# Two-layer MLA/SSD/pooling backbone: a fixed bias tile, an earlier band load and a new order around the pooling of layer 1

## The chip, the cores and the metric

The kernel runs on one core of one Trainium2 chip. The metric is the device time of one execution in microseconds (us). The engines are named as in the profile: PE (TensorE matmuls) and PEld (its weight loads), DVE (VectorE), ACT (ScalarE), POOL (GpSimd) and SP (SyncE). In this kernel SP only issues DMAs, and ACT issues some DMAs in between its own work, so that a DMA of ACT's that has to wait holds up ACT.

## The reference

Two layers over 640 tokens of width 1024: 128 context tokens and 512 latent tokens. Layer 0 mixes tokens by latent attention and a two-way state space scan, layer 1 by pooling with four windows. Each layer ends in a SwiGLU network (the FFN) of hidden width 2816. Shifts, scales and gates of every part come from conditioning vectors. Cut to what the change touches:

```
def modulation(cvec, w_mod, b_mod):
    m = jnp.expand_dims(jax.nn.silu(cvec) @ w_mod + b_mod, -2)
    return split_last(m, (D_MODEL,) * 6)

def modulate(x, g, shift, scale):
    return rmsnorm(x, g) * (1 + scale) + shift

def pool_mixer(h, w_pool, pool_scale):
    for gi, w in enumerate(POOL_WINDOWS):          # 2, 4, 8, 16
        lo = np.clip(t - w // 2, 0, L)
        hi = np.clip(t + w // 2, 0, L)
        ...
        outs.append(mean - hf[..., gi * POOL_GC:(gi + 1) * POOL_GC])
    out = jnp.einsum('blgc,gcd->blgd', pooled, w_pool).reshape(b, L, d)
    return out * pool_scale

def swiglu(h, w_gate, w_up, w_down):
    return (jax.nn.silu(h @ w_gate) * (h @ w_up)) @ w_down

    for l in range(DEPTH):
        ...
        xs = xs + g_s * rmsnorm(mix_s, norm_post_mix[l])
        fs = swiglu(modulate(xs, norm_pre_ffn[l], shf_s, scf_s), ffn_w_gate[l], ffn_w_up[l], ffn_w_down[l])
        xs = xs + gf_s * rmsnorm(fs, norm_post_ffn[l])
```

Outputs are the tokens after both layers, and the new latent keys and scan states of layer 0.

## The kernel before

Tokens stand in five tiles of 128: tile 0 is the context, tiles 1 to 4 the latent grid. All matmuls of the FFN split each operand into a high and a low part (h = rounded copy, l = rest) and add three products. The splits are work for other engines: ACT writes the high part (L89, L421, L589), DVE or POOL subtract to get the low part (L90, L422, L590).

The program runs in this order: layer 0's mixer (to about 475 us), FFN 0 (to about 909), the transition with the whole mixer of layer 1 (to about 990), FFN 1, and the last residual.

**FFN.** Each FFN works through 11 pairs of a gate and an up block of 256 hidden columns; each block is a `Matrix`. A matrix is multiplied with seven products in place of eight (Strassen's way): p1 to p7 (L515, with weights `a1h`, `a2h` and the like from the tokens, and `ha`, `hc`, `la`, `lc` and the like from the matrix). POOL forms the sums of quarters that this needs (`adds`, L485 to L488), ACT and DVE split them (`hw`/`lw`, `hc`/`lc`, ...). Pair 0 runs ahead (`plain`, `first`), in the plain form for what the transposed tokens allow and in the seven-product form for the rest; in the code below, `seq` holds the other 20 matrices, and each iteration of the loop over `seq` does one matrix `m`, prepares the next (`nx.load`, `nx.a`, `nx.adds`, `nx.c`, `nx.b`, `nx.d`), and, between the products, runs five tiles of the down projection of the pair before (`down_add`, L97 to L99 with weights `hw`, `lw` and the tokens' `ah`, `al`). In an iteration PE's order is p1, p2, p5, p6, two down tiles, p7, a down tile, and so on. `p6` overwrites the PSUM tile that `act`'s copy at L549 (an ACT instruction) has to have read before. `out_split` writes `ah` on ACT (L589) and `al` on POOL (L590).

**Background rows.** While an FFN runs, a generator `net.bg` computes the gates of later residuals (silu(c) times w_mod, plus b_mod) on DVE, a few instructions at each call: `mod_gate_mac` loads 512 KB pieces `mraw` and adds them up in `macc` (L275). The first addition takes the bias from a tile `bb`: zeros in all rows but the first, which holds a row of `b_mod`. POOL clears `bb` (L263), and then ACT issues the DMA of row 0 (L264). This is done for six half-gates: four in FFN 0, two in FFN 1.

**Transition.** `finish0` takes the finished FFN tiles one after the other: last down tiles on PE, sum on DVE (L612), norm and gate (L350 to L353 and L365, writing the residual `xs`), the norm of the next mixer (L311, L316, writing `hn`). From `hn`, `pool_in(tt)` computes a pooled tile on PE: the window means are a product of `hn` with a banded matrix, `band` (1056 KB), for the tile itself, with eight columns for the overlap with the tile in front and eight for the tile behind (L1354). The results go through ACT and DVE (L1361, L1359, writing `pf`, with a per-channel factor and an offset `mv`). `mix(tt)` multiplies `pf` by the pool weights (L1658) and does the residual, its norm (writing `y`) and leaves a function that transposes `y` (`tr`, L332) for FFN 1. PE's order is set by hand: `after` puts pool 0, mix 0, pool 1, mix 1 and pool 2 between the FFN tails of tiles 1 to 4, and `rest` does what is left. The offset's factor needs column sums of `band`: `_band_shift` reduces `band` on DVE to `rs` (L1369), a PE matmul with ones adds it over the partitions (L1371), and eight small DVE instructions write `mv` (L1374).

Within each engine the order of instructions is what a scheduler of the framework makes of the program; DMAs of SP and ACT stand in those engines' orders.

## Time and profile before

| | |
|---|---|
| runs | 1447.77, 1449.42, 1452.63 us; median 1449.42 |
| the profiled execution | 1448.13 us |
| its span in the trace | 1446.3 us, mean granted clock of PE 0.978 |
| PE | 1370.3 us busy (95%), 7914 matmuls |
| DVE | 984.5 us busy (68%) |
| ACT | 639.0 us busy (44%) |
| POOL | 415.9 us busy (29%) |
| DMA | 165.45 MB, 114 GB/s on average |

PE is busy nearly all the time, so the page alone says little; the timelines of single stretches show where it is not. Times in the trace start at the span's start. In rows of the timeline, the number in brackets is the idle time of that engine ahead of the instruction and what ended it. The granted clock is that of PE: 1.00 is its full level of 2.4 GHz, and a stretch at half that is 1.2 GHz. The matmuls of pooling and mixing appear as two records each.

### The profile page before, as it was taken

Reading aid. Unit: us, or ns where it says so; the run is one execution under the profiler, and the core shown is the slowest. Engines: PE = TensorE matmul, PEld = TensorE weight load, DVE = VectorE, ACT = ScalarE, POOL = GpSimd, SP = SyncE. Lnnn points to the kernel's source line nnn. Section 1 sums busy time; section 2 is a strip of 40 time slices with the busy share of each in tenths; the row PEclk is TensorE's granted clock in tenths of the full one; section 3 lists DMA queues with packets and bytes.
Section 4 is the critical chain, followed back from the end, with each engine's and each line's share of the span. In section 5 each row is a group of like instructions: output and inputs, shape, how many; then the busy total and the mean of one; then the engine's idle time right before and its main releaser. Section 6 shows DMA issues by size and latency. Waiting matters only on the chain.

```text
span 1446.3 us, 20387 instructions
## 1 busy us (share of the span) xinstructions
PE 1370.3 (95%) x7914; PEld 1172.8 (81%) x7914; DVE 984.5 (68%) x1468; ACT 639.0 (44%) x1140; POOL 415.9 (29%) x349
## 2 busy tenths in 40 slices
PE   5999999999999889999999999797899999999997
PEld 2788765576658879989989998687889989999996
DVE  3755547767836886786877865666876776666557
ACT  3544644753414644334333334467444343343433
POOL 0000034253400353424343333002533333333320
PEclk8999999989999999999999999899999999999999
DMA  9434345600063243232332325320242323222213
GB/s 371 129 124 143 117 136 196 225 15 15 30 198 122 95 144 100 85 131 88 111 115 83 116 88 177 145 88 30 96 131 88 105 81 115 88 88 88 86 46 145
DMA packets 50276, 165.45 MB, mean 114 GB/s; under 512 B 5938, under 2 KB 9522, under 8 KB 50052
## 3 DMA queue, kind: packets, MB, share of 16 engines
q1 hardware_dynamic: 43344, 153.96, 32.0%
q10 hardware_dynamic: 6836, 10.19, 2.2%
q8 instruction: 62, 1.02, 0.3%
q14 instruction: 34, 0.28, 0.1%
HBM read 155.57 MB, written 8.56 MB: 113 GB/s over the span
## 4 chain that ended last, share of the span: by engine, by line
PE 74%; DVE 10%; DMA 6%; issue 4%; ACT 3%; POOL 2%; POOLq 0%; ACTq 0%; DVEq 0%; SPq 0%
PE ps L515 26%; PE ps L97 11%; PE ps L99 11%; PE ps L98 11%; DMA mraw<-in_w_mod 3%; PE ps L179 3%; DVE macc L275 3%; PE ps L1354 2%; PE ps L1255 1%; PE ps L1658 1%; PE ps L1237 1%; DMA band<-in_band 1%; PE ps L1217 1%; PE ps L1238 1%; PE ps L1239 1%
## 5 line engine op out<-in xcount | busy, mean ns | idle before, releaser
L485 POOL TENSOR_TENSOR q<-raw,raw 128x512 f32<-128x512 f32 x40 | 54.9, 1372 | 362.7 <-DMA raw<-in_w_up 117.2
L99 PE MATMUL ps<-hw,al 128*128 128x512 f32 x380 | 151.2, 398 | 1.8 <-POOL al L590 1.8
L97 PE MATMUL ps<-hw,ah 128*128 128x512 f32 x380 | 151.5, 399 | 0.8 <-ACT ah L589 0.8
L98 PE MATMUL ps<-lw,ah 128*128 128x512 f32 x380 | 151.3, 398 | 0.0
L612 DVE TENSOR_TENSOR y<-y,ps 128x512 f32<-128x512 f32 x180 | 121.1, 683 | 39.1 <-PE ps L99 36.5
L515 PE MATMUL ps<-a2h,hc 128*128 128x320 f32 x320 | 100.8, 315 | 12.2 <-ACT sg L549 12.2
L590 POOL TENSOR_TENSOR al<-sg,ah 128x640 fp32r<-128x640 f32 x42 | 78.2, 1861 | 92.5 <-ACT ah L589 83.8
L515 PE MATMUL ps<-a2h,hb 128*128 128x320 f32 x320 | 99.5, 311 | 1.8 <-ACT sg L559 1.2
L515 PE MATMUL ps<-a2h,lc 128*128 128x320 f32 x320 | 100.1, 313 | 0.0
L515 PE MATMUL ps<-a2l,hc 128*128 128x320 f32 x320 | 100.1, 313 | 0.0
L515 PE MATMUL ps<-a1h,la 128*128 128x320 f32 x320 | 99.0, 309 | 0.2 <-DVE la L90 0.2
L515 PE MATMUL ps<-a1h,ha 128*128 128x320 f32 x320 | 98.9, 309 | 0.0
L515 PE MATMUL ps<-a1l,ha 128*128 128x320 f32 x320 | 98.8, 309 | 0.0
L515 PE MATMUL ps<-a2l,hb 128*128 128x320 f32 x320 | 98.8, 309 | 0.0
L515 PE MATMUL ps<-a2h,lb 128*128 128x320 f32 x320 | 98.8, 309 | 0.0
L275 DVE SCALAR_TENSOR_TENSOR macc<-mraw,silc,macc 128x512 f32<-128x512 f32 x84 | 79.3, 972 | 28.0 <-DMA mraw<-in_w_mod 28.0
L99 PEld LDWEIGHTS ps<-hw,al 128*128 128x128 f32 x380 | 71.9, 189 | 19.7 <-POOL al L590 2.6
L488 POOL TENSOR_TENSOR t<-raw,q 128x512 f32<-128x512 f32 x40 | 58.5, 1464 | 100.0 <-DVE ld L90 65.8
L97 PEld LDWEIGHTS ps<-hw,ah 128*128 128x128 f32 x380 | 72.4, 191 | 13.7 <-ACT ah L589 1.7
L98 PEld LDWEIGHTS ps<-lw,ah 128*128 128x128 f32 x380 | 72.2, 190 | 12.2
L89 ACT ACTIVATE hd<-t 128x512 fp32r<-128x512 f32 x40 | 25.3, 632 | 120.6 <-PE ps L515 105.9
L90 DVE TENSOR_TENSOR lc<-q,hc 128x1024 fp32r<-128x1024 f32 x40 | 48.9, 1222 | 37.5 <-ACT hc L89 37.3
(445 smaller groups left out, 3943.5 us busy)
## 6 DMA issues: line engine op xcount, KB each, us to landing
raw<-in_w_mod SPq DMA_DIRECT2D x56, 512.0 KB
raw<-in_w_gate SPq DMA_DIRECT2D x44, 512.0 KB
raw<-in_w_up SPq DMA_DIRECT2D x44, 512.0 KB
raw<-in_w_down SPq DMA_DIRECT2D x44, 512.0 KB
mraw<-in_w_mod SPq DMA_DIRECT2D x40, 512.0 KB
xs<-xd SPq DMA_DIRECT2D x10, 512.0 KB
x<-in_x_sample SPq DMA_DIRECT2D x8, 512.0 KB
raw<-in_w_xbc SPq DMA_DIRECT2D x8, 512.0 KB
```

Source lines behind the costliest of these rows:

```text
L90: (eng or self.nc.vector).tensor_tensor(l, x, h.bitcast(F32), ALU.subtract)
L97: mm(out, ah, bh, start=first and i == 0, stop=False)
L98: mm(out, ah, bl, start=False, stop=False)
L99: mm(out, al, bh, start=False, stop=last and i == n - 1)
L179: nc.tensor.matmul(out[32 * g : 32 * g + 32], self.silc[:, kc], x[:, k2 * 512 : k2 * 512 + 512], start=kc < 4, stop=kc >= 4,)
L275: nc.vector.scalar_tensor_tensor(acc[:, v], x[:, k2 * 512 : k2 * 512 + 512], self.silc[:, kc, v : v + 1], acc[:, v] if kc else bb, op0=ALU ...
L485: g.tensor_tensor(self.q[:, lo], self.rb[:, lo], self.ra[:, lo], ALU.subtract)
L488: g.tensor_tensor(self.t4, self.ra[:, hi], self.q[:, hi], ALU.subtract)
L515: mm(out, x[:, k], z[:, k], start=first and n == 0, stop=n == len(terms) - 1, skip_group_check=True)
L590: (eng or nc.gpsimd).tensor_tensor(al, g.s[:, f], ah.bitcast(F32), ALU.subtract)
L612: nc.vector.tensor_tensor(yd, yd, out, ALU.add)
L1354: nc.tensor.matmul(o, x, m, start=i == 0, stop=i == len(mats) - 1, skip_group_check=True)
```

## The change

- The bias tile `bb` is made once for each layer, cleared by DVE in front of the pair loop, and each half-gate only loads its row 0.
- In the pair loop, the splits of a matrix's b and d quarters (`m.b()`, `m.d()`) move from the iteration before into the matrix's own iteration, behind p2 and behind p6. `A.fourth()`, the last of the sums of tokens, moves into the first iteration.
- The load of `band` goes from ACT's queue to SP's, in the program behind the residuals of tiles 0 and 1. The second gate tile is loaded behind it.
- The column sums of `band` come with an input (columns 40 to 43 of `bvec`), so that the DVE reduction goes and `_band_shift` needs no band.
- The eight columns for the tile behind are left out for the first two channel chunks (the pooling window of 2 has no reach behind it).
- In `rest`, mix 2 stands ahead of pool 3, and the transposes stand elsewhere.

```
-        bb = self.mrp.tile([P, 512], F32, tag="bb", name=self.name("bb"), bufs=1)
+        bb = self.bb
...
-        nc.gpsimd.memset(bb, 0.0)
...
+    net.bb = net.mrp.tile([P, 512], F32, name=net.name("bb"))
+    nc.vector.memset(net.bb, 0.0)
...
-    n1.b()
-    n1.d()
-    A.fourth()
...
         w.p2()
+        m.b()
...
         w.p6()
+        m.d()
         if nx:
             nx.a()
         d()
+        if n == 2:
+            A.fourth()
...
-        if nx:
-            nx.b()
-            nx.d()
...
-            if 0 < tt < NT - 1:
+            if 0 < tt < NT - 1 and dc >= 2:
...
-    rs = net.small.tile([P, 4], F32, tag="rs", name=net.name("rs"), bufs=1)
-    nc.vector.tensor_reduce(rs, band[:, :, 3 * P : 4 * P], axis=AX.X, op=ALU.add)
     tot = net.pt([P, 4])
-    nc.tensor.matmul(tot, net.cm[:, CM_ONE], rs, start=True, stop=True)
+    nc.tensor.matmul(tot, net.cm[:, CM_ONE], net.bc[:, 40:44], start=True, stop=True)
...
-        xs = x_back(ts.enter_context(pool("xs", "left")), 0)
-        g1 = net.gate_load(ts.enter_context(pool("gp", "left")), gd[1])
...
-        nc.scalar.dma_start(band, t["band"])
+        for tt in range(NT):
+            nc.sync.dma_start(xs[:, tt], xd[0, tt])
+            if tt == 1:
+                nc.sync.dma_start(band, t["band"])
+        g1 = net.gate_load(gp, gd[1])
...
-        ab = [a]
+        ab = a, _band_shift(net, m1[0])
...
         def rest():
+            trs.pop(0)()
+            mix(2)
             pool_in(3)
-            mix(2)
             trs.pop(0)()
             pool_in(4)
             mix(3)
-            trs.pop(0)()
             trs.pop(0)()
             mix(4)
             return trs
...
+    L["bvec"] = np.concatenate([bvec, bd[:, :, 3 * P : 4 * P].sum(-1)], 1)
```

How the order of the engines changes is shown at three places. Line numbers of the changed kernel are one or two lower there.

**The start of FFN 0's pair loop.** ACT before, from the first row-0 load of `bb` to the split of the first matrix's a quarter (`ha`):

```order
L264 DMA bb_4893<-in_b_mod 1x512
L89 ACTIVATE hb_4805<-raw_4729 128x1024
L630 ACTIVATE sg_4470<-ps_4745 128x320
L421 ACTIVATE a2h_4460<-y 128x1280
L89 ACTIVATE hw_4817<-raw_4815 128x1024
L264 DMA bb_5669<-in_b_mod 1x512
L549 ACTIVATE sg_4821<-ps_4826 128x320
L589 ACTIVATE ah_4801<-sg_4470 128x640
L89 ACTIVATE ha_4881<-raw_4822 128x1024
```

and ACT now:

```order
L263 DMA bb_4727<-in_b_mod 1x512
L629 ACTIVATE sg_4470<-ps_4747 128x320
L89 ACTIVATE hb_4847<-raw_4731 128x1024
L420 ACTIVATE a2h_4460<-y 128x1280
L89 ACTIVATE hw_4809<-raw_4807 128x1024
L588 ACTIVATE ah_4803<-sg_4470 128x640
L548 ACTIVATE sg_4813<-ps_4818 128x320
L89 ACTIVATE ha_4881<-raw_4814 128x1024
L540 ACTIVATE sg_4813<-sg_4813 128x320
L263 DMA bb_4727<-in_b_mod 1x512
```

The second load of `bb` no longer stands between `hw` and the copy that p6 needs (L549, now L548), but behind `ha`; the `ah` of the down projection now stands ahead of that copy. On DVE, at the same place, the rows before were

```order
L90 TENSOR_TENSOR lb_4806<-raw_4729,hb_4805 128x1024
L275 SCALAR_TENSOR_TENSOR macc_4898<-mraw_4899,silc,bb_4893 128x512 x2
L422 TENSOR_TENSOR a2l_4461<-y,a2h_4460 128x1280
L632 TENSOR_TENSOR sg_4470<-sg_4470,ps_4775 128x320
L90 TENSOR_TENSOR lw_4818<-raw_4815,hw_4817 128x1024
```

and are now

```order
L651 MEMSET bb_4727 128x512
L90 TENSOR_TENSOR lb_4848<-raw_4731,hb_4847 128x1024
L274 SCALAR_TENSOR_TENSOR macc_4896<-mraw_4897,silc,bb_4727 128x512
L631 TENSOR_TENSOR sg_4470<-sg_4470,ps_4777 128x320
L421 TENSOR_TENSOR a2l_4461<-y,a2h_4460 128x1280
L90 TENSOR_TENSOR lw_4810<-raw_4807,hw_4809 128x1024
```

The sum on which `ah` waits (L632, now L631) moved ahead of the long `a2l`, and one of the two background additions moved behind `lw`.

**The first tails of the transition.** DVE, from the sums of the FFN tiles 0 and 1 (`y`) to the residual of tile 0, before:

```order
L612 TENSOR_TENSOR y<-y,ps_8424 128x512
L612 TENSOR_TENSOR y<-y,ps_8444 128x512
L351 TENSOR_TENSOR junk_8438<-y,G_8379 128x512 x2
L612 TENSOR_TENSOR y<-y,ps_8474 128x512
L351 TENSOR_TENSOR junk_8488<-y,G_8379 128x512
L353 TENSOR_SCALAR ss_1491_8439<-ss_1491_8439 128x1
L612 TENSOR_TENSOR y<-y,ps_8494 128x512
L351 TENSOR_TENSOR junk_8488<-y,G_8379 128x512
L1369 TENSOR_REDUCE rs_8524<-band 128x4
L105 RECIPROCAL r_8462<-sd_8461 128x1
L1374 TENSOR_SCALAR mv_8528<-mv_1567,ps_8526 128x2
L365 SCALAR_TENSOR_TENSOR xs_8385<-junk_8438,r_8462,xs_8385 128x512 x2
```

and now:

```order
L611 TENSOR_TENSOR y<-y,ps_8429 128x512
L611 TENSOR_TENSOR y<-y,ps_8449 128x512
L350 TENSOR_TENSOR junk_8443<-y,G_8373 128x512
L352 TENSOR_SCALAR ss_1489_8444<-ss_1489_8444 128x1
L350 TENSOR_TENSOR junk_8443<-y,G_8373 128x512
L611 TENSOR_TENSOR y<-y,ps_8479 128x512
L350 TENSOR_TENSOR junk_8493<-y,G_8373 128x512
L105 RECIPROCAL r_8467<-sd_8466 128x1
L364 SCALAR_TENSOR_TENSOR xs<-junk_8443,r_8467,xs 128x512 x2
```

The reduction of `band` is gone, the eight `mv` instructions stand some 15 rows earlier, and the residual of tile 0 (L365, now L364) stands ahead of the second half of tile 1.

**The end of the transition.** PE in `rest`, from the third mix to the first matmul of FFN 1 (`a1h,ha`), before (L1658 is a mix, L332 a transpose):

```order
L1658 MATMUL ps_8959<-q_8411,pf_8843 128x256 x4
L1658 MATMUL ps_8969<-t_1487_8412,pf_8843 128x256 x2
L1658 MATMUL ps_8969<-hd_8413,pf_8843 128x256 x2
L332 MATMUL ps_8991<-cm,y 128x128 x4
L332 MATMUL ps_9000<-cm,y 128x128 x4
L332 MATMUL ps_9011<-cm,y 128x128 x4
L332 MATMUL ps_9020<-cm,y 128x128 x4
L1658 MATMUL ps_9032<-q_8411,pf_8931 128x256 x4
L1658 MATMUL ps_9042<-t_1487_8412,pf_8931 128x256 x2
L1658 MATMUL ps_9042<-hd_8413,pf_8931 128x256 x2
L97 MATMUL ps_9093<-a1h,ha_9089 128x320
```

and now, from the last matmuls of mix 2 (the 16 rows of pool 4 between the transposes of tile 1 and mix 3 are left out):

```order
L1656 MATMUL ps_8862<-hd_8407,pf_8789 128x256 x2
L331 MATMUL ps_8917<-cm,y 128x128 x4
L331 MATMUL ps_8926<-cm,y 128x128 x4
L1352 MATMUL ps_8938<-band,hn 128x128
...
L1352 MATMUL ps_8951<-band,hn 128x8
L1656 MATMUL ps_8965<-q_8405,pf_8884 128x256 x3
L1656 MATMUL ps_8975<-t_1483_8406,pf_8884 128x256
L1656 MATMUL ps_8965<-q_8405,pf_8884 128x256
L1656 MATMUL ps_8975<-t_1483_8406,pf_8884 128x256
L1656 MATMUL ps_8975<-hd_8407,pf_8884 128x256 x2
L331 MATMUL ps_8997<-cm,y 128x128 x4
```

Before, the transposes of tiles 1 and 2 stood back to back behind mix 3; now pool 4 and mix 3 stand between them. Before mix 3, pool 4's matmuls had been mixed with those of mix 2.

## Rows read from the trace of the kernel before

**Rows 1.** The page: busy time of each engine.

```profile
...
PE 1370.3 (95%) x7914; PEld 1172.8 (81%) x7914; DVE 984.5 (68%) x1468; ACT 639.0 (44%) x1140; POOL 415.9 (29%) x349
...
```

**Rows 2.** Windows of two steady stretches of FFN 0 (columns: busy time by engine, granted clock).

```profile
...
540.00:559.30 19.30, 19.30 (x116) 17.85 (x116) 12.51 (x16) 9.69 (x16) 6.67 (x5) 1.00 0.38 116
...
```

**Rows 3.** Waits of PE from 478 to 1420 us (total, times, longest).

```profile
...
PE ps L515 <- ACT sg L549: 12.2, 5, 6.4
...
PE ps L1371 <- DVE rs L1369: 3.2, 1, 3.2
...
```

**Rows 4.** Timeline around the start of FFN 0's pair loop.

```profile
...
506.65 0.53 ACTq L264 DMA_DIRECT2D bb<-in_b_mod  x1
...
510.19 3.09 DVE L275 SCALAR_TENSOR_TENSOR macc<-mraw,silc,bb 128x512 f32<-128x512 f32 x2 [0.29 <-DMA bb<-in_b_mod]
...
514.36 2.51 POOL L488 TENSOR_TENSOR t<-raw,q 128x512 f32<-128x512 f32 x1
...
516.07 1.88 DVE L90 TENSOR_TENSOR lw<-raw,hw 128x1024 fp32r<-128x1024 f32 x1
...
517.64 0.44 ACT L549 ACTIVATE sg<-ps 128x320 f32<-128x320 f32 x1 [6.86 <-POOL bb L263]
...
518.13 0.64 PE L515 MATMUL ps<-a2h,hc 128*128 128x320 f32 x1 [6.43 <-ACT sg L549]
...
518.78 1.56 POOL L590 TENSOR_TENSOR al<-sg,ah 128x640 fp32r<-128x640 f32 x1 [1.45 <-ACT ah L589]
...
523.44 0.39 PE L99 MATMUL ps<-hw,al 128*128 128x512 f32 x1
...
```

**Rows 5.** Timeline around the start of FFN 1's pair loop.

```profile
...
1030.12 1.54 POOL L590 TENSOR_TENSOR al<-sg,ah 128x640 fp32r<-128x640 f32 x1
...
1030.55 1.06 ACT L89 ACTIVATE hw<-raw 128x1024 fp32r<-128x1024 f32 x1 [6.56 <-POOL bb L263]
...
1032.61 0.63 PE L515 MATMUL ps<-a2h,hc 128*128 128x320 f32 x1 [4.64 <-ACT sg L549]
...
1038.54 0.44 PE L97 MATMUL ps<-hw,ah 128*128 128x512 f32 x1
...
```

**Rows 6.** Timeline around the residual, norm and pooling of tile 0.

```profile
...
910.21 0.30 ACT L104 ACTIVATE sd<-ss 128x1 f32<-128x1 f32 x1
...
912.10 0.69 DVE L1369 TENSOR_REDUCE rs<-band 128x4 f32<-128x512 f32 x1 [1.04 <-DMA band<-in_band]
...
913.61 1.41 DVE L365 SCALAR_TENSOR_TENSOR xs<-junk,r,xs 128x512 f32<-128x512 f32 x2
...
917.69 3.78 PE L1354 MATMUL ps<-band,hn 128*128 128x128 f32 x16 [4.26 <-DVE hn L316]
...
```

**Rows 7.** PE's timeline in the rest of the transition.

```profile
...
936.55 3.63 PE L1354 MATMUL ps<-band,hn 128*128 128x128 f32 x32
...
967.78 1.95 PE L1354 MATMUL ps<-band,hn 128*128 128x8 f32 x16
969.57 0.60 PE L1658 MATMUL ps<-hd,pf 128*128 128x256 f32 x2
...
978.31 1.09 PE L332 MATMUL ps<-cm,y 128*128 128x128 f32 x8 [2.70 <-DVE y L316]
979.23 1.89 PE L1658 MATMUL ps<-q,pf 128*128 128x256 f32 x8
...
986.95 0.42 PE L97 MATMUL ps<-a1h,ha 128*128 128x320 f32 x1 [4.09 <-DVE a1h L432]
...
989.49 0.63 PE L98 MATMUL ps<-a1l,ha 128*128 128x320 f32 x1 [0.80 <-DVE a1l L433]
...
```

**Rows 8.** The page: POOL's last add of a matrix, over the program.

```profile
...
L488 POOL TENSOR_TENSOR t<-raw,q 128x512 f32<-128x512 f32 x40 | 58.5, 1464 | 100.0 <-DVE ld L90 65.8
...
```

**Rows 9.** Issues on SP's queue around the residual loads.

```profile
...
898.91 2.57 SPq L1604 DMA_DIRECT2D xs<-xd  x5
...
```

**Rows 10.** DVE's timeline where the residual of tile 3 is used.

```profile
...
941.28 1.41 DVE L365 SCALAR_TENSOR_TENSOR xs<-junk,r,xs 128x512 f32<-128x512 f32 x2
...
```

More of the change, by code (lines that the diff above doesn't have):

```diff
@@ L130, in setup @@
         nc.scalar.dma_start(self.pv, t["pvec"])
-        self.bc = b.tile([P, 40], F32, name="bc")
+        self.bc = b.tile([P, 44], F32, name="bc")
         nc.scalar.dma_start(self.bc, t["bvec"])
@@ L1362, in _pool_tile, with _band_shift @@
     return pf
-def _band_shift(net, band, b):
+def _band_shift(net, b):
     nc = net.nc
-    rs = net.small.tile([P, 4], F32, tag="rs", name=net.name("rs"), bufs=1)
-    nc.vector.tensor_reduce(rs, band[:, :, 3 * P : 4 * P], axis=AX.X, op=ALU.add)
     tot = net.pt([P, 4])
-    nc.tensor.matmul(tot, net.cm[:, CM_ONE], rs, start=True, stop=True)
+    nc.tensor.matmul(tot, net.cm[:, CM_ONE], net.bc[:, 40:44], start=True, stop=True)
     bz = net.mod_vec_tile()
@@ L1630, in finish0 @@
         g = net.gate_load(right, gd[0])
-        xs = x_back(ts.enter_context(pool("xs", "left")), 0)
-        g1 = net.gate_load(ts.enter_context(pool("gp", "left")), gd[1])
+        xs = ts.enter_context(pool("xs", "left")).tile([P, NT, D], F32, name="xs")
+        gp = ts.enter_context(pool("gp", "left"))
         net.work = net.dp = ts.enter_context(pool("workt", "left", 2))
@@ L1644, in pool_in @@
         def pool_in(tt):
-            if len(ab) == 1:
-                ab.append(_band_shift(net, band, m1[0]))
             pfs[tt] = _pool_tile(net, pp, band, hn, tt, ab)
@@ L1754, in _layout @@
         "ssd_dt_bias_fwd", "ssd_dt_bias_bwd", "ssd_a_log_fwd", "ssd_a_log_bwd", "ssd_d")]
-    L["bvec"] = np.broadcast_to(np.concatenate(bv), (P, 40))
+    bvec = np.broadcast_to(np.concatenate(bv), (P, 40))
     r = np.arange(P)
```

## The prediction, made before the changed kernel was timed

> **What bounds the kernel now.** I read the page first: PE is busy for 95% of the span, the next engine, DVE, for 68% [rows 1]. In a window over a whole matrix of FFN 0, PE is busy for 19.30 of 19.30 us at the full clock of 1.00 with 116 matmuls, 0.166 us each [rows 2]. There a change on another engine gains nothing. So only the stretches matter in which PE stands still or runs at its lower level. The list of PE's waits by what ended them is headed by products waiting for ACT's copy at L549: 12.2 us in five waits, the longest 6.4 [rows 3]. The timelines place the waits at four spots.
>
> At the start of FFN 0's loop PE idles 6.43 us before p6 (518.13). ACT had been idle 6.86 us and was released by POOL's clearing of `bb`; the last of POOL's adds, ahead of it, ended at 516.87 [rows 4]. FFN 1 repeats this: ACT held 6.56 us at `hw`, PE 4.64 us before p6 [rows 5]. In the transition PE idles 4.26 us before pool 0, with 3.23 us of the column sums' wait ahead of that, nearly without work between [rows 3, 6]. In `rest`, PE waits 2.70 us for the transposes of tile 2, and 4.09 and 0.80 us at the first matmuls of FFN 1 [rows 7].
>
> PE restarts at half clock after the long ones. At FFN 0, 17 matmuls took from 518.13 to 523.44, 5.3 us [rows 4], where 17 times 0.166 is 2.8: the clock costs 2.5 us more. At FFN 1 it is 18 in 5.9 us [rows 5], 2.9 us more. Pool 0's first 16 records took 3.78 us, where 32 such took 3.63 later, so 2.0 us more. After the wait of 2.70 the transposes, eight in 1.09 us, show no such loss [rows 6, 7].
>
> **Start of FFN 0.** The second load of `bb` leaves the place between `hw` and L549, and nothing on ACT waits for POOL's adds. What is late next: L549 now stands behind `ah`, which waits for DVE's L632. On DVE this comes behind `lb` and one addition into `macc`, no longer behind two and `a2l`. The first addition waits for `bb`'s row. That load now waits for DVE's clearing of `bb` (about 508) and I give it 3.5 us from issue, as before (506.65 to 510.19). With 1.5 us, half of the two of before, the addition ends near 512.9 [rows 4], L632 near 513.3, L549 near 514.4, and p6 starts about 514.6, 3.5 us earlier and after a wait of about 3, which may or may not cost the clock. Down tile 0 follows; it needs `lw`, which ended at 517.95 [rows 4] and comes at about 517.4, and `al` of the second half, which POOL can only start after its adds at 516.87; with 1.56 us [rows 4] it is there at 518.4. The tile ends near 519.0 instead of 523.7, 4.7 us earlier. I take off one us, because the background additions moved back now stand ahead of later splits: **3.7 us**. Bounds: 0 and 8.9 (the whole 6.43 and the clock's 2.5).
>
> **Start of FFN 1.** The same, without a late `ah`: ACT is free at 1024.0, so L549 and p6 have no wait. Down tile 0 then waits for POOL: the adds end at about 1029.6, 0.5 us of clearing before the first `al` goes, `al` takes 1.54 us, a second as much: 1032.8. The tile ends near 1033.3; before, it ended where the next began, at 1038.54 [rows 5]. That is 5 us and more; with some half-clock time left, **4.8 us** (0 to 7.5, the 4.64 and the clock's 2.9).
>
> **Pool 0.** The reduction of `band`, its matmul and the eight `mv` instructions leave the path; early, in the last matrix, they lie beside PE's full stretch. The residual of tile 0 then needs only its own norm: ACT's `sd` ends at 910.51, so it starts at about 910.7 and not 913.61; the rest of the chain, `hn` and pool 0, keeps its 4.1 us to 917.69 [rows 6]. Pool 0 starts 2.9 us earlier, a little more as the `ss` of tile 0 moved forward: **3.2 us** (0, if `band` lands late; 7.5, both waits). The half clock stays, since PE still idles near 5 us. Moving the load itself I cost at nothing: `band` had landed by 912.10 [rows 6], and is not needed before 914.
>
> The Trainium skill (DMA: Bandwidth & Descriptors, section "Issuing engines are not separate DMA queues") says that DMAs from different engines run on the same 16 DMA engines and interleave, and that a second issuer only saves the time of issuing. By this, too, the sum for the move of the load is 0; no run here shows it yet.
>
> **Eight columns left out.** Two chunks in three tiles, two records each: 12 records at 1.95 us for 16 [rows 7], **1.5 us** (0, where PE waits anyway, to 2.9 at half clock).
>
> **The order in `rest`.** From mix 2's end (970.17) to tile 2's transposes (978.31) the chain over norm, residual and `y` takes 8.1 us [rows 7]. Now the transposes of tile 1 (1.1), pool 4 (32 records, 3.7 to 3.9 by the same row) and mix 3 (16 records, where eight took 1.89 at 979.23: 3.5) stand between: 8.4. The wait of 2.70 goes. At the start of FFN 1, before, DVE reached the `a1h` of tile 2 only after the split of tiles 0 and 1; that is now done while pool 4 runs. I expect the 4.89 us of waits to fall to about 1.2, and the clock's cost (about 2.5, as at the FFN starts) to go with them. All of it would be 2.7 + 3.7 + 2.5 = 8.9. As the transposes, residual and cast of tile 2 keep the same work on ACT and DVE, I take two thirds: **6.0 us**. Bounds: 9.9 (all waits 7.6 and most of the clock), and -2.7, a wait of the same length in front of mix 2, whose `pf` now has less time.
>
> The moved splits (b, d, fourth) I cost at nothing: the steady matrices keep PE at 19.30 of 19.30 us, with DVE at 12.51 of it [rows 2]; without that cover each would cost its own 1.2 us.
>
> **Sum.** 3.7 + 4.8 + 3.2 + 1.5 + 6.0 = 19.2. The profiled execution took 1448.13 us (span 1446.3), so 1428.9; the median of the runs is 1.29 above the profiled one: **1430.2 us**.
>
> **Rivals.**
>
> *The waits come back behind POOL and DVE.* Every start then hangs on `lw`, `al` or the cast of tile 2. For it: POOL's last add took 2.51 us at FFN 0 [rows 4] against a mean of 1.46 [rows 8], and `lw` took 1.88 [rows 4]; both are needed now. Against: that slowness is already in my times. It would give 1.5 at FFN 0, 2.0 at FFN 1, 3.2, 0.8, and 2.7 in `rest`, 10.2 together: 1439.2 us.
>
> The Trainium skill (SBUF — State Buffer, section "SBUF: two separate sides") has a rule that speaks for this: the port pair that VectorE and GpSimd share is locked for a whole instruction when a VectorE operation with two SBUF inputs meets a GpSimd one that reads SBUF. The 2.51 us agree in direction. By it the adds would be no faster with the row load gone, and `al` as late as this rival has it: 1439.2 again.
>
> *More than forecast.* Of `rest` all 9.9, and both FFN starts without clock loss (4.7 and 5.5): about 1424.6 us. For it: no wait of the list has another cause than those named.
>
> *The change doesn't do what it says:* ACT waits elsewhere, for example the second row load for DVE's reading of the one `bb`, now a shared tile, ahead of `hc`. With the starts at nothing and `rest` at nothing, 4.7 remain at most, and half of that, lost at pool 0 to `band`, gives 1447.
>
> *Slower: SP held at `band`.* It now stands on SP ahead of two residuals and the first `w_up` loads of FFN 1, and additionally waits for DVE. SP issued the residuals at 898.91 to 901.48 [rows 9]. Tile 3's is used at 941.28 [rows 10], some 6 us earlier with the gains ahead of it. If the memory of `band` came free only late, each us beyond about 930 (a 2.6 us load of `band` and the residuals behind it) delays everything by one; beyond 954 it eats the whole sum and the limit of 0.3%. Against: the DVE work in that place is FFN 0's, which ends near 904.
>
> **Chances.** Forecast (1425 to 1435.5): 0.52. Waits come back (1435.5 to 1445): 0.26. More (below 1425): 0.08. No change: 0.07. Slower: 0.07, of which SP 0.04 and the rest for what I don't see. About 0.3% (4.3 us) is what a measurement of this kernel can tell from no change. Faster by more than that is the first three: 0.86; within it 0.07; slower 0.07. The range of 1423.5 to 1442.5 leaves out the slow end of the second case (0.05), the fast end of the third (0.03) and the last two, 0.22 or a little less.
>
> **What would show it.** L549 within 3 us of `hw`, p6 of FFN 0 near 514.6 and down tile 0 ended near 519; p6 of FFN 1 without a wait; pool 0 about 4 to 5 us behind the last tail; no 2.7 us wait ahead of transposes, and the first `a1h,ha` matmul with a wait near 1 us at full clock. Wrong it would be above all if PE's wait list shows new entries for `lw`, `al` or `pf` of some 3 us each, or if SP stops at `band`.

## The result

The changed kernel takes 1434.58 us (median of 4 runs, 1432.96 to 1436.75) against 1449.7 us before (4 runs, 1447.77 to 1452.63): the ratio is 0.9892, 95% interval 0.9868 to 0.9917, so 15.1 us or 1.1% faster. The forecast was 1430.2, range 1423.5 to 1442.5.

The profiled execution took 1432.96 us, with a span of 1431.2. The page's line of busy times, which answers to [rows 1]:

```profile
...
PE 1364.6 (95%) x7902; PEld 1165.0 (81%) x7902; DVE 984.9 (69%) x1469; ACT 638.3 (45%) x1140; POOL 417.1 (29%) x343
...
```

PE is busy for 5.7 us less, and the span is 15.1 shorter: the larger part is idle time that went. The list of PE's waits of the changed kernel from 478 to 1420 us (total, number, longest), which answers to [rows 3]:

```profile
...
PE ps L99 <- POOL al L589: 7.1, 6, 3.6
PE ps L514 <- ACT sg L548: 5.0, 3, 2.7
PE ps L1352 <- DVE hn L315: 4.0, 1, 4.0
PE ps L97 <- DVE a1h L431: 2.1, 1, 2.1
...
PE ps L98 <- DVE lw L90: 1.3, 2, 1.0
...
PE ps L98 <- DVE a1l L432: 1.2, 1, 1.2
...
```

The wait for the column sums is gone, and the wait for L549 (now L548) has shrunk from 12.2 to 5.0 us. In its place there are waits for `al` on POOL, 7.1 us with a longest of 3.6, where there had been 3.3 in all, and for `lw`.

**Where it came from, stage by stage.** Both kernels run the same products on PE in the same order, so the start of the same product can be compared. The columns give the time between such marks in the profiled execution of each kernel: 1 is from FFN 0's first seven-product matmul (L515, L514 after) to its 217th (the start of the loop), 2 on to nearly the last product of FFN 0's pairs (the 1657th of 1680), 3 to the first matmul of pool 0, 4 to the last tail matmul of FFN 0 (L97), 5 to the first seven-product matmul of FFN 1, 6 to its 145th, 7 to nearly its last. "First" is where the first product itself starts. The kernels below "changed" are those of the experiments.

| kernel | first | 1 | 2 | 3 | 4 | 5 | 6 | 7 | 1 to 7 |
|---|---|---|---|---|---|---|---|---|---|
| before | 506.3 | 57.4 | 331.4 | 22.6 | 27.3 | 77.5 | 43.9 | 342.4 | 902.5 |
| changed | 504.7 | 58.5 | 331.4 | 18.5 | 26.2 | 69.6 | 42.3 | 342.5 | 888.9 |
| undo_bb | 507.8 | 57.3 | 333.6 | 18.4 | 26.2 | 67.9 | 42.0 | 342.7 | 888.1 |
| bb_alone | 506.2 | 59.1 | 331.1 | 23.2 | 26.6 | 76.0 | 44.3 | 342.2 | 902.4 |
| undo_rest | 502.9 | 58.5 | 331.6 | 18.5 | 26.2 | 76.3 | 40.5 | 342.5 | 894.0 |
| rest_alone | 508.6 | 57.6 | 331.0 | 22.6 | 27.7 | 72.1 | 42.3 | 342.4 | 895.7 |
| undo_shift | 507.6 | 57.9 | 330.9 | 19.1 | 27.1 | 69.5 | 41.7 | 342.6 | 888.8 |
| undo_band | 504.9 | 59.0 | 331.6 | 20.2 | 27.3 | 69.6 | 42.7 | 342.6 | 892.9 |
| undo_splits | 505.1 | 59.3 | 331.4 | 18.5 | 26.2 | 67.9 | 43.1 | 342.8 | 889.3 |
| bg_late | 508.9 | 59.2 | 336.8 | 18.4 | 27.4 | 72.1 | 42.6 | 341.2 | 897.6 |
| al_dve | 501.4 | 59.5 | 331.8 | 18.5 | 26.0 | 67.9 | 42.6 | 342.6 | 888.9 |
| halves | 506.0 | 59.8 | 339.3 | 18.4 | 27.4 | 68.7 | 43.6 | 342.0 | 899.0 |
| halves_undo_bb | 503.3 | 58.3 | 339.9 | 19.5 | 27.0 | 69.5 | 40.6 | 345.4 | 900.1 |
| no_first | 506.4 | 55.0 | 333.0 | 18.4 | 26.1 | 71.2 | 42.0 | 342.7 | 888.5 |

The column "first" differs by up to 7.5 us among kernels whose edits leave the mixer of layer 0 alone: that is what single executions differ by, and 1.5 of the 15.1 us between the two profiled executions are of this kind. Each row is one execution, and the stages scatter as well. Among the kernels that leave a stage as it is in the changed kernel, stage 1 takes 57.9 to 59.0 us (undo_rest, undo_shift, undo_band), stage 4 26.0 to 27.4 (al_dve, bg_late, halves), stage 5 67.9 to 72.1 (undo_bb, bg_late) and stage 6 41.7 to 42.7 (undo_shift, undo_band); stage 3 is 18.4 or 18.5 in all of them but halves_undo_bb. A difference within such a spread tells nothing by itself.

From the first product on, the change is worth 13.6 us: nothing but a loss at FFN 0 (1.1), 4.1 ahead of pool 0, 1.1 between the FFN tails (within the spread), 7.9 in the rest of the transition and pair 0 of FFN 1, 1.6 at the start of FFN 1's loop.

**The start of FFN 0.** The timeline of the changed kernel there, which answers to [rows 4]:

```profile
...
509.56 1.77 DVE L274 SCALAR_TENSOR_TENSOR macc<-mraw,silc,bb 128x512 f32<-128x512 f32 x1
...
512.41 0.42 ACT L548 ACTIVATE sg<-ps 128x320 f32<-128x320 f32 x1
512.42 2.56 POOL L487 TENSOR_TENSOR t<-raw,q 128x512 f32<-128x512 f32 x1
...
512.88 0.42 PE L514 MATMUL ps<-a2h,hc 128*128 128x320 f32 x1 [2.70 <-ACT sg L548]
...
513.73 2.33 DVE L90 TENSOR_TENSOR lw<-raw,hw 128x1024 fp32r<-128x1024 f32 x1
...
517.53 0.50 PE L99 MATMUL ps<-hw,al 128*128 128x512 f32 x1 [0.22 <-POOL al L589]
...
```

ACT's copy (L548) no longer waits for POOL, PE waits 2.70 us in front of p6 instead of 6.43, and runs on at full clock. Since `first` differs by 1.5, p6 is 3.7 us earlier. From the first product to the 49th it is 15.5 us, 18.8 before. But the same kernel loses it 17 us later. The timeline of the changed kernel from 532 to 542 us:

```profile
...
533.76 2.07 DVE L274 SCALAR_TENSOR_TENSOR macc<-mraw,silc,macc 128x512 f32<-128x512 f32 x3 [3.02 <-DMA mraw<-in_w_mod]
...
535.76 0.48 DVE L575 TENSOR_TENSOR sg<-sg,ps 128x320 f32<-128x320 f32 x1
...
536.27 0.74 ACT L577 ACTIVATE sg<-sg 128x640 f32<-128x640 f32 x1 [5.05 <-DVE sg L575]
536.91 0.42 ACT L548 ACTIVATE sg<-ps 128x320 f32<-128x320 f32 x1
...
537.38 0.42 PE L514 MATMUL ps<-a2h,hc 128*128 128x320 f32 x1 [1.84 <-ACT sg L548]
...
539.61 0.63 PE L97 MATMUL ps<-hw,ah 128*128 128x512 f32 x1
...
```

DVE has just waited 3.02 us for a piece of `mraw`, does three additions of the background row, and only then the sum L575; ACT's silu (L577) waits for it 5.05 us, the copy L548 stands behind that, and PE's p6 of the second matrix waits 1.84 us for the copy. Some 1.4 us later PE falls to half clock for a while (granted clock 0.50 from 538.8 to 542.0, matmuls of 0.63 us; the down matmuls behind 542 take 0.40 again). From the 49th to the 145th product it is 28.1 us, 23.9 before. DVE's timeline of the kernel before has the same sum (L576 there) just as late:

```profile
...
532.19 2.08 DVE L275 SCALAR_TENSOR_TENSOR macc<-mraw,silc,macc 128x512 f32<-128x512 f32 x3 [3.42 <-DMA mraw<-in_w_mod]
...
536.58 0.48 DVE L576 TENSOR_TENSOR sg<-sg,ps 128x320 f32<-128x320 f32 x1
...
```

**The transition.** The timeline of the changed kernel around the residual and pool 0, which answers to [rows 6]:

```profile
...
908.57 1.41 DVE L364 SCALAR_TENSOR_TENSOR xs<-junk,r,xs 128x512 f32<-128x512 f32 x2
...
910.07 1.06 ACT L310 ACTIVATE hn<-xs 128x1024 f32<-128x1024 f32 x1 [1.12 <-issue]
...
913.12 2.79 PE L1352 MATMUL ps<-band,hn 128*128 128x128 f32 x16 [3.95 <-DVE hn L315]
...
```

The residual of tile 0 (L364) starts at 908.57, 5.0 us earlier than the 913.61 of before, and pool 0 4.6 us earlier, after one wait of 3.95 us; measured from the end of stage 2, the two are 4.6 and 4.1 us earlier. In `rest` (PE's timeline, answers to [rows 7]):

```profile
...
943.46 4.97 PE L1352 MATMUL ps<-band,hn 128*128 128x128 f32 x44
...
967.48 1.06 PE L331 MATMUL ps<-cm,y 128*128 128x128 f32 x8
...
974.12 0.39 PE L97 MATMUL ps<-a1h,ha 128*128 128x320 f32 x1 [2.13 <-DVE a1h L431]
975.71 0.64 PE L98 MATMUL ps<-a1l,ha 128*128 128x320 f32 x1 [1.19 <-DVE a1l L432]
...
```

The transposes of tile 2 (967.48) have no wait, pool 2's 44 records took 4.97 us, and `a1h` and `a1l` are waited for 2.13 and 1.19 us. The clock's cost at the start of FFN 1 is not all gone: the granted clock from 974 to 978 is 0.71.

**The start of FFN 1** (timeline, answers to [rows 5]):

```profile
...
1007.52 1.61 POOL L589 TENSOR_TENSOR al<-sg,ah 128x640 fp32r<-128x640 f32 x1 [2.97 <-ACT ah L588]
...
1007.59 2.62 DVE L90 TENSOR_TENSOR lc<-q,hc 128x1024 fp32r<-128x1024 f32 x1
...
1010.29 2.72 POOL L484 TENSOR_TENSOR q<-raw,raw 128x512 f32<-128x512 f32 x1 [1.17 <-DVE lc L90]
...
1019.40 1.98 POOL L589 TENSOR_TENSOR al<-sg,ah 128x640 fp32r<-128x640 f32 x1
...
1021.43 0.79 PE L99 MATMUL ps<-hw,al 128*128 128x512 f32 x1 [3.56 <-POOL al L589]
...
```

DVE's timeline of the kernel before has this `lc` at

```profile
...
1019.75 1.22 DVE L90 TENSOR_TENSOR lc<-q,hc 128x1024 fp32r<-128x1024 f32 x1
...
```

There is now no wait in front of p6 at all, but one of 3.56 us for `al` of the second half, behind POOL's adds, and half clock after it (granted clock 0.51 from 1023 to 1027; 0.79 us for the first matmul).

### The profile page after: what moved, and what is told of

Same layout as the page of the kernel before. It is cut to its first block, busy times and chain, and to the rows that moved or that the text cites. A ratio compares the mean times of both kernels' runs of the same rounds, so it can differ in the third digit from the quotient of the medians.

```text
span 1431.2 us, 20363 instructions
## 1 busy us (share of the span) xinstructions
PE 1364.6 (95%) x7902; PEld 1165.0 (81%) x7902; DVE 984.9 (69%) x1469; ACT 638.3 (45%) x1140; POOL 417.1 (29%) x343
## 4 chain that ended last, share of the span: by engine, by line
PE 74%; DVE 12%; DMA 6%; issue 4%; ACT 3%; POOL 1%; POOLq 0%; DVEq 0%; ACTq 0%; SPq 0%
PE ps L514 25%; PE ps L97 11%; PE ps L99 11%; PE ps L98 11%; DMA mraw<-in_w_mod 5%; DVE macc L274 4%; PE ps L179 4%; PE ps L1253 1%; PE ps L1352 1%; PE ps L1656 1%; DVE lw L90 1%; PE ps L1061 1%; DMA raw<-in_w_mod 1%; PE ps L1235 1%; PE ps L1215 1%
## 5 line engine op out<-in xcount | busy, mean ns | idle before, releaser
L97 PE MATMUL ps<-hw,ah 128*128 128x512 f32 x380 | 151.9, 400 | 0.9 <-ACT ah L588 0.9
L589 POOL TENSOR_TENSOR al<-sg,ah 128x640 fp32r<-128x640 f32 x42 | 81.3, 1935 | 89.6 <-ACT ah L588 81.8
L514 PE MATMUL ps<-a2h,hc 128*128 128x320 f32 x320 | 99.6, 311 | 5.1 <-ACT sg L548 5.0
L514 PE MATMUL ps<-a2h,hb 128*128 128x320 f32 x320 | 100.0, 313 | 2.9 <-ACT sg L558 2.0
L274 DVE SCALAR_TENSOR_TENSOR macc<-mraw,silc,macc 128x512 f32<-128x512 f32 x84 | 78.6, 966 | 32.8 <-DMA mraw<-in_w_mod 32.8
L514 PE MATMUL ps<-a2l,hb 128*128 128x320 f32 x320 | 99.3, 310 | 0.0
L514 PE MATMUL ps<-a2h,lb 128*128 128x320 f32 x320 | 99.2, 310 | 0.0
L514 PE MATMUL ps<-a1h,la 128*128 128x320 f32 x320 | 99.0, 309 | 0.2 <-DVE la L90 0.2
L514 PE MATMUL ps<-a2h,lc 128*128 128x320 f32 x320 | 99.0, 310 | 0.0
L514 PE MATMUL ps<-a2l,hc 128*128 128x320 f32 x320 | 99.0, 309 | 0.0
L514 PE MATMUL ps<-a1h,ha 128*128 128x320 f32 x320 | 98.9, 309 | 0.0
L514 PE MATMUL ps<-a1l,ha 128*128 128x320 f32 x320 | 98.8, 309 | 0.0
L97 PEld LDWEIGHTS ps<-hw,ah 128*128 128x128 f32 x380 | 72.4, 191 | 13.6 <-ACT ah L588 1.8
```

The source lines that it names most:

```text
L97: mm(out, ah, bh, start=first and i == 0, stop=False)
L274: nc.vector.scalar_tensor_tensor(acc[:, v], x[:, k2 * 512 : k2 * 512 + 512], self.silc[:, kc, v : v + 1], acc[:, v] if kc else bb, op0=ALU ...
L514: mm(out, x[:, k], z[:, k], start=first and n == 0, stop=n == len(terms) - 1, skip_group_check=True)
L589: (eng or nc.gpsimd).tensor_tensor(al, g.s[:, f], ah.bitcast(F32), ALU.subtract)
```

## The experiments

Times are medians of the runs of each kernel; the changed kernel has 1434.58. A ratio is to runs of the kernel before on the same chip. Stages are those of the table.

**undo_bb**: the bias tile cleared by POOL for each half-gate again.

```
-        bb = self.bb
+        bb = self.mrp.tile([P, 512], F32, tag="bb", name=self.name("bb"), bufs=1)
...
+        nc.gpsimd.memset(bb, 0.0)
...
-    net.bb = net.mrp.tile([P, 512], F32, name=net.name("bb"))
-    nc.vector.memset(net.bb, 0.0)
```

> The changed kernel with the bias tile cleared by POOL for each half-gate, as before. Theory A (what the two traces side by side show: the 3.3 us that the changed kernel had gained by the eighth product block of FFN 0 are lost again by 548 us, to background additions on DVE that wait for their weights; at FFN 1 only 1.6 us are gained): the time rises by 1 to 2 us to about 1436, the wait of 6 us in front of p6 of FFN 0 comes back, and FFN 0 ends no later for it. Theory B (the recorded prediction: 3.7 us at FFN 0 and 4.8 at FFN 1): it rises by 8.5 us to about 1443.

1434.89 us, ratio 0.9886 (0.9860 to 0.9912). The wait of p6 at FFN 0 is back, in PE's timeline of this kernel:

```profile
...
519.66 0.63 PE L515 MATMUL ps<-a2h,hc 128*128 128x320 f32 x1 [6.42 <-ACT sg L549]
...
```

Yet stage 1 takes 57.3 us, 1.2 less than with the fixed tile; stage 2 takes 2.2 more, and stage 5 1.7 less, by the clock alone (last section). At FFN 1 (stage 6, 42.0) nothing comes back either: without the fixed tile, the scheduler's order there no longer has the long stall. The fixed tile is worth nothing that these runs can tell (0.3 us between the medians). Theory A has it so, though its rise of 1 to 2 us didn't come; theory B falls.

**bb_alone**: the kernel before with the fixed tile alone (the same edit, the other way round).

> The kernel before with the fixed bias tile alone. Theory A: at FFN 0 the gain is lost by 550 us, at FFN 1 a few microseconds are kept if POOL's al comes earlier than in the changed kernel: 1446 to 1449. Theory B (the recorded terms of 3.7 and 4.8): 1441.

1450.56 us, ratio 1.0007 (0.9986 to 1.0028): no change. PE's wait in front of p6 at FFN 0 is down from 6.43 us to 2.58:

```profile
...
514.24 0.42 PE L514 MATMUL ps<-a2h,hc 128*128 128x320 f32 x1 [2.58 <-ACT sg L548]
...
```

Yet stage 1 takes 59.1 us, 1.7 more than before, and stage 6 44.3, 0.4 more. Theory B falls. Theory A holds at FFN 0; at FFN 1 nothing is kept either, and p6 there still waits 2.50 us.

**undo_rest**: the old order in `rest`.

```
         def rest():
-            trs.pop(0)()
-            mix(2)
             pool_in(3)
+            mix(2)
             trs.pop(0)()
             pool_in(4)
             mix(3)
+            trs.pop(0)()
             trs.pop(0)()
             mix(4)
```

> The changed kernel with the old order in rest. Theory A (between pool 2 and the first matmuls of FFN 1 the traces differ by 8.0 us, of which half a microsecond is left-out columns): the time rises by 7 to 8 us to about 1442, with a wait of 2 to 3 us for the transposes of tile 2 and one of about 4 us at the first matmul of FFN 1. Theory B (the recorded term): by 6.0 us, to 1440.6. If the gain came from the earlier offset factors and not from the order, it stays near 1435.

1438.87 us over runs from 1436.23 to 1449.04, ratio 0.9925 (0.9898 to 0.9952), 4.3 us more in the median, less than either theory. The trace gives 6.7 us more in stage 5, with the wait at FFN 1's first matmul at its longest in any kernel here:

```profile
...
980.23 0.60 PE L97 MATMUL ps<-a1h,ha 128*128 128x320 f32 x1 [6.98 <-DVE a1h L431]
...
```

and 1.8 us less in stage 6, 4.9 in all.

**rest_alone**: the kernel before with the new order in `rest` alone (the same edit, the other way round).

> The kernel before with the new order in rest alone. Theory A (7 to 8 us by the traces): about 1442. Theory B (recorded 6.0): 1443.7. If the order only pays together with the earlier pool 0, less than 3 us: 1447.

1440.98 us, ratio 0.9927 (0.9904 to 0.9949), 8.0 us less than before. In the trace, stage 5 gains 5.4 us and stage 6 1.5. This one edit is about half of the whole change (8.0 of 15.1 us by the runs, 6.9 of 13.6 by the stages), and at FFN 1 it brings about what the changed kernel gains there, without the fixed tile. POOL's timeline of this kernel and, below it, of the kernel before show how:

```profile
...
1019.68 0.53 POOL L263 MEMSET bb<- 128x512 f32 x1
1020.91 2.21 POOL L485 TENSOR_TENSOR q<-raw,raw 128x512 f32<-128x512 f32 x1 [0.70 <-DVE lc L90]
...
```

```profile
...
1029.64 0.52 POOL L263 MEMSET bb<- 128x512 f32 x1
...
```

POOL now clears `bb` 0.2 us behind FFN 1's first product and ahead of its adds; before, it did so 7.1 us behind that product, after the adds. So ACT's load of the row, and `hw` behind it, no longer wait for the adds. undo_bb has POOL's order of rest_alone there.

**undo_shift**: the column sums of `band` by DVE again, in front of pool 0.

```
...
-    tot = net.pt([P, 4])
-    nc.tensor.matmul(tot, net.cm[:, CM_ONE], net.bc[:, 40:44], start=True, stop=True)
+    rs = net.small.tile([P, 4], F32, tag="rs", name=net.name("rs"), bufs=1)
+    nc.vector.tensor_reduce(rs, band[:, :, 3 * P : 4 * P], axis=AX.X, op=ALU.add)
+    tot = net.pt([P, 4])
+    nc.tensor.matmul(tot, net.cm[:, CM_ONE], rs, start=True, stop=True)
...
-        ab = a, _band_shift(net, m1[0])
+        ab = [a]
...
         def pool_in(tt):
+            if len(ab) == 1:
+                ab.append(_band_shift(net, band, m1[0]))
```

> The changed kernel with the column sums of band taken by DVE again, in front of pool 0. Theory A (pool 0 gained 5.1 us between the traces): the time rises by 4 to 5 us to about 1439. Theory B (the recorded term): by 3.2 us to 1437.8. If instead the earlier landing of band brought it, nearly nothing: DVE would then reduce at once and the time stays within 1 us.

1435.51 us, ratio 0.9895 (0.9870 to 0.9921). Stages 3 and 4 take 0.6 and 0.9 us more; the second is within the spread. DVE's timeline of this kernel:

```profile
...
910.17 1.41 DVE L364 SCALAR_TENSOR_TENSOR xs<-junk,r,xs 128x512 f32<-128x512 f32 x2
...
912.81 0.69 DVE L1367 TENSOR_REDUCE rs<-band 128x4 f32<-128x512 f32 x1 [0.57 <-DMA band<-in_band]
...
```

The reduction still waits for `band` (until 912.81; measured from the end of stage 2 that is half a microsecond earlier than before), but the residual of tile 0 stands ahead of it in DVE's order, not behind it. So neither theory holds: in this order the reduction costs 0.6 us ahead of pool 0.

**undo_band**: the load of `band` on ACT's queue again.

```
-            if tt == 1:
-                nc.sync.dma_start(band, t["band"])
         g1 = net.gate_load(gp, gd[1])
+        nc.scalar.dma_start(band, t["band"])
```

> The changed kernel with the load of band on ACT's queue behind the two gate loads, as before, all else changed. Nothing of it moves on PE; on DVE the residual of tile 0 stands again behind both halves of tile 1, three instructions of 0.7 us later. Theory A (of the 4.1 us that pool 0 starts earlier, the place of the residual in DVE's order brings most, and the queue brings that order through the scheduler): pool 0 starts 1.5 to 2.5 us later than in the changed kernel, the time is about 1436.5. Theory B (the column sums' wait was all: moving the load is worth nothing, as recorded): pool 0 starts as in the changed kernel, and the time stays near 1435.

1440.02 us, ratio 0.9929 (0.9913 to 0.9945), 5.4 us more than the changed kernel in the median and 4.0 in the sum of the stages: 1.7 of it in stage 3, the rest in stages that scatter as much. DVE's timeline of this kernel and, below it, PE's:

```profile
...
910.02 0.69 DVE L611 TENSOR_TENSOR y<-y,ps 128x512 f32<-128x512 f32 x1 [0.80 <-PE ps L99]
...
911.54 1.42 DVE L364 SCALAR_TENSOR_TENSOR xs<-junk,r,xs 128x512 f32<-128x512 f32 x2
...
```

```profile
...
915.63 3.78 PE L1352 MATMUL ps<-band,hn 128*128 128x128 f32 x16 [5.65 <-DVE hn L315]
...
```

The residual (L364) stands behind both halves of tile 1 again, whose last comes at 910.02, when the last tail matmul lets it. Theory A for pool 0, which starts 1.7 us later; the move of the load does bring time, through the order of another engine. Against the kernel before, pool 0 is still 2.4 us earlier here (20.2 us in stage 3 against 22.6). What no longer stands ahead of the residual on DVE is the reduction with its wait: with the residual behind both halves of tile 1, taking it away is worth 2.4 us by this comparison.

**undo_splits**: the b and d splits and `A.fourth()` at their old places (the loop's part of the diff undone).

> The changed kernel with the splits of the b and d quarters in the iteration before and the last token sums ahead of the loop, as before. Both theories: 0 within 1 us in the steady matrices. A rival, that the moved splits put the background additions of FFN 0 in a worse place and so cause the loss there: FFN 0 ends 3 us earlier and the time falls to about 1431.5.

1435.05 us, ratio 0.9890 (0.9857 to 0.9924). Stage 2, the steady matrices, is the same (331.4). Stages 1 and 6 take 0.8 and 0.9 us more, hardly outside the spread: the moved splits don't cause the loss, and a gain by them at the starts is not shown.

**al_dve**: one subtraction moved from POOL to DVE.

```
-    at0.append(out_split(Out(s0), 1))
+    at0.append(out_split(Out(s0), 1, nc.vector))
```

> The changed kernel with one subtraction moved from POOL to DVE: the low part (al) of pair 0's second half. Theory A (at the start of FFN 1 PE waits 3.56 us for this al, which POOL does behind four adds of 9.1 us): that wait goes, FFN 1's start gains 2 to 3 us, and the time falls to about 1432; at FFN 0 PE waited only 0.22 us for it, so nothing there. Theory B (lw or la on DVE, now behind one more subtraction of 1 to 2 us, holds PE in its place): the time stays within 1 us of 1434.6.

1438.73 us over runs from 1429.57 to 1441.89, ratio 0.9899 (0.9869 to 0.9929); the sum of the stages of its profiled execution (1429.57 us), 888.9, is that of the changed kernel. PE's waits of this kernel from 1000 to 1060 us:

```profile
...
PE ps L514 <- ACT sg L558: 2.4, 1, 2.4
PE ps L514 <- ACT sg L566: 2.2, 1, 2.2
PE ps L99 <- DVE al L589: 0.6, 1, 0.6
...
```

The wait for `al` fell from 3.6 to 0.6 us, and two others took its place, for copies of ACT's (the one at L566 was 1.3 us in the changed kernel); stage 6 takes 42.6 us, as in the changed kernel (42.3). Theory B in its outcome, though it is not `lw` that PE waits for.

**bg_late**: the background rows one matrix later.

```
-            net.bg()
+            if n > 2:
+                net.bg()
```

> The changed kernel, whose background rows (the additions on DVE that wait for 512 KB pieces of w_mod) start one matrix later in each FFN: no net.bg() in the loop's first iteration. Theory A (in the changed kernel's first three matrices DVE stands 3 us at a time at an addition that waits for its piece, and the copies for PE queue behind it; the waits of PE of 1.84 us and a stretch at half clock behind it give the start's gain back): the loss between 530 and 548 us goes, FFN 0 ends 3 us earlier, and the time falls by about 3 us to 1431.5; the stall may also just move one matrix on, which a wait near 555 us would show. Theory B (FFN 0 is held by the loads of its own weights, whatever DVE does): the lead is lost at the same place and the time stays at 1434.6.

1437.23 us, ratio 0.9905 (0.9876 to 0.9935). This settles nothing on the start: the scheduler left the first additions where they were, and stage 1 takes 59.2 us with much the same waits. Stage 2 takes 5.4 us more in the profiled execution (1445.81 us, well above the median).

**halves**: `w_mod` in pieces of 256 KB into two half-size buffers.

```
...
+        def piece(kc):
+            x = self.mrp.tile([P, 512], F32, tag="mraw", name=self.name("mraw"), bufs=2)
+            c = (kc % 2) * 512
+            nc.sync.dma_start(x, self.t["w_mod"][l, 2 * j + half, kc // 2][:, c : c + 512])
+            return x
+
+        q = [piece(0), piece(1)]
+        for kc in range(8):
...
+            if kc < 6:
+                q.append(piece(kc + 2))
```

> The changed kernel, whose background rows load w_mod in pieces of 256 KB into two buffers of half the size, in place of 512 KB into one: the next piece loads while DVE adds the one before. Theory A (the lead at FFN 0 is lost because DVE waits some 3 us at an addition for its piece, three times between 525 and 548 us): these waits fall below 1 us, FFN 0 keeps about 3 us of its lead at the first product of the fifth matrix, and the time falls by 3 to 4 us to about 1431. Theory B (the matrices' own weights hold the start): the lead is lost again by 550 us, with PE waiting for hw, ha or the adds, and the time stays at 1434.6.

1444.34 us, ratio 0.9960 (0.9946 to 0.9973), 9.8 us slower than the changed kernel. DVE's timeline and PE's waits of this kernel:

```profile
...
531.43 1.41 DVE L278 SCALAR_TENSOR_TENSOR macc<-mraw,silc,macc 128x512 f32<-128x512 f32 x2 [0.28 <-DMA mraw<-in_w_mod]
533.94 0.75 DVE L278 SCALAR_TENSOR_TENSOR macc<-mraw,silc,macc 128x512 f32<-128x512 f32 x1 [1.10 <-DMA mraw<-in_w_mod]
...
538.73 0.47 DVE L580 TENSOR_TENSOR sg<-sg,ps 128x320 f32<-128x320 f32 x1
...
```

```profile
...
PE ps L519 <- ACT sg L553: 3.8, 1, 3.8
```

DVE's waits for the pieces fell to 1.1 us and less, as theory A has it, and the lead was lost all the same: with the pieces there sooner, the scheduler put fifteen additions ahead of the sum (L580 here, the L575 above) in place of eleven; it came at 538.73, 32.8 us behind the first product, and PE waited 3.8 us. Theory A fails as it stood, since the waits for pieces are not the whole cause; of theory B there is no sign either, as no wait for weights shows. In stage 2 it loses 7.9 us more.

**halves_undo_bb**: the same pieces, and the bias tile cleared by POOL.

> The same half pieces in two buffers, but with the bias tile cleared by POOL for each half-gate. Theory A: the wait in front of p6 of FFN 0 (6 us) stays, and nothing is waiting for the pieces that PE feels; the start of FFN 0 takes as long as before (57.4 us from its first product to the 217th), so that the fixed tile shows its 3 to 4 us only against this kernel: 1435. Theory B: both kernels with half pieces agree at 550 us.

1441.46 us, ratio 0.9940 (0.9925 to 0.9955). Stage 1 takes 58.3 us, with the wait in front of p6 at 6.25 us; with the fixed tile (halves) it takes 59.8. The 3 to 4 us of theory A don't come: again the fixed tile shows no gain.

**no_first**: of the first background row of FFN 0 only the first piece of w_mod is loaded and added.

```
         for u in range(4):
+            if u and (l, j, half) == (0, 5, 0):
+                for _ in range(4):
+                    yield
+                continue
```

> The changed kernel without three quarters of the first background row of FFN 0: of the first half-gate's four pieces of w_mod only the first is loaded and added (4 additions on DVE in place of 16), so that gate is wrong in this kernel. On DVE the order up to the third addition is that of the changed kernel; behind it no addition stands ahead of the sums and splits of the first two matrices. Theory A (the lead of 3.3 us at FFN 0 is lost because the background additions, ten of them with two pieces to wait for, stand on DVE ahead of the sum that PE's p6 of the second matrix waits for through ACT): the wait of 1.84 us at that p6 and the half clock behind it go, and FFN 0's first five matrices take 3 to 5 us less than in the changed kernel, 54 us against 58.5 from product 0 to product 216; the time falls to about 1431. Theory B (the matrices' own weights, POOL's adds or their splits hold the start): the lead is lost all the same by product 144, and the time stays at 1434.6.

1432.67 us, ratio 0.9894 (0.9873 to 0.9914). PE's waits from 505 to 560 us are these four, none of them behind 523 us:

```profile
...
PE ps L518 <- ACT sg L552: 2.7, 1, 2.7
PE ps L518 <- ACT sg L562: 1.7, 1, 1.7
PE ps L98 <- DVE lw L90: 1.0, 1, 1.0
PE ps L99 <- POOL al L593: 0.2, 1, 0.2
```

and on DVE the sum (L579 here) comes earlier:

```profile
...
533.59 0.48 DVE L579 TENSOR_TENSOR sg<-sg,ps 128x320 f32<-128x320 f32 x1
...
```

Stage 1 takes 55.0 us, 3.5 less than in the changed kernel and 2.4 less than before: from the 49th to the 145th product it is 23.9 us, as before, and the lead of the start stays. So the background row holds DVE and through it PE, loads and additions together (this kernel drops both, and so doesn't tell one from the other). The time does not show the lead: the ratio is that of the changed kernel (0.9892). 1.6 us are lost again in stage 2, most of them at its end, where PE waits 1.1 us for `lc`, and 1.6 in stage 5, within its spread. Theory A holds for stage 1, its 1431 is not shown.

## Why the prediction was right, and where it was not

The sum, 19.2 us, was 15.1 by the runs and 13.6 by the stages; the way there was partly another.

- **Start of FFN 0** (3.7, measured -1.1): mis-sized, and this is the step that failed most. "L549 near 514.4, and p6 starts about 514.6, 3.5 us earlier" held: p6 came 3.7 us earlier, and the down tile waited for `lw` and `al` as worked out (0.98 and 0.22 us). "I take off one us, because the background additions moved back" was the right place with the wrong size: all of it was given back, and more. In DVE's order the last sum of the loop's first matrix stands behind background additions and the pieces that they wait for, twelve additions before and eleven after; it comes 30.3 us behind the first product before (536.58 in the trace) and 31.0 after (535.76). PE now was early for it. Before, the stall in front of p6 had hidden this second limit. That it is the background row, and not the matrices' weights or splits, is shown by no_first, where the sum comes at 27.1 us (533.59). Shorter waits for its pieces did not release it in halves, where more additions stood ahead of the sum.
- **Start of FFN 1** (4.8, measured 1.6): the first rival came true here. PE waits 3.56 us for `al`, which ends 12.5 us behind the first product of FFN 1 (1021.38), 11.8 before; the prediction had it at 10.3 (1032.8 in the trace of before). This is the sign of being wrong that it named. The stall in front of p6 did go, but not by the fixed tile: undo_bb and rest_alone show 1.9 and 1.5 us in that stage without it. POOL started its adds 2.9 us later than before, against the first product, and they wait for `lc` on DVE. That starts 1.5 us later, by DVE's order, and takes 1.4 us more: 2.62 us, while POOL ran its `al` beside it, from 1007.52. The 38 `lc` of this trace that ran with POOL idle took 1.21 to 1.23 us each. The Trainium skill (SBUF — State Buffer, section "SBUF: two separate sides") states that of a VectorE operation with two SBUF inputs and a GpSimd one that reads SBUF, the first to start holds the port pair that the two share for its whole instruction, while the other is blocked. The trace agrees in direction, with 2.62 us against 1.22.
- **Pool 0** (3.2, measured 4.1 in stage 3): right in size, by the predicted way in part. Without the reduction, and with the residual in its old place, pool 0 starts 2.4 us earlier (undo_band against before), where the prediction had 2.9 for it. The other 1.7 come from the load's move, which it "cost at nothing" (undo_band against the changed kernel). Put back behind the residual, the reduction costs only 0.6 (undo_shift): what it is worth hangs on the order. `band` landed half a microsecond earlier, and nothing waits for that; the scheduler, with the load off ACT's queue, put tile 0's residual ahead of the second half of tile 1 on DVE. The order that stands ahead of the prediction shows exactly this row, and I gave it only 0.3 us ("a little more").
- **Eight columns** (1.5): pool 1 took 3.63 us with 32 records [rows 7] and 3.19 with 28 (931.27 in the changed kernel), 0.44 for four; 1.3 for the three tiles, an estimate from the one. Right by this; no run undoes this edit alone.
- **The order in `rest`** (6.0; stage 5 gained 7.9, of which some 0.9 are columns): right, within the stage's spread. undo_rest gives 6.7, rest_alone 5.4. The wait of 2.70 us went, and the 4.89 at FFN 1's start fell to 3.32, not to 1.2. Some 1.7 of the 7.9 are less half clock behind the pooling (3.4 us before, 1.7 after, last section), which no term had and which differs between kernels of the same order: as far as these runs show, luck.
- **Splits** (nothing): 0 in the steady matrices; at the two starts 0.8 and 0.9 us, which are not clear of the spread.
- **SP held at `band`** and **no change**: didn't come. SP issued `band` (900.35) and all five residuals without a pause, from 898.47 to 901.88.

The two misses at the FFN starts (4.8 and 3.2 us too much) and the gains from the order of the transition's instructions partly cancelled, so that the time came out within the range. That is in part luck: the two terms that rest on the fixed tile, 8.5 of the 19.2 us, gave 0.5 in the stages, and not by that tile.

When only `rest` changes, the stall at FFN 1 goes because POOL clears `bb` ahead of its adds there (rest_alone); why the scheduler then orders it so is open. No version here beats the changed kernel by more than its runs scatter, not even no_first, which leaves work out.

## What to carry to other kernels

A stall that is taken away is worth only what the next wait in the order leaves: compare, for each engine behind it, when its instructions come against a common mark, not only where PE waits now. Background work that a scheduler deals out over an in-order engine is such a wait; it doesn't show among PE's waits in the trace of before as long as an earlier stall covers it. And where a scheduler makes the order, an edit that costs nothing by itself (a load on another queue) may move rows on another engine: read the order of the changed program for each edit alone.
